# Two more Strassen units in the first up group of a one-layer decoder kernel, and another schedule for the early weight sums

## The chip, the core and the metric

The kernel runs on one core of one Trainium2 chip. The core has engines that work side by side, each through its own instructions in their order: PE (TensorE, matrix products), DVE (VectorE), ACT (ScalarE), POOL (GpSimd) and SP (SyncE), of which the last is used here to start DMA transfers. The metric is the device time of one execution in microseconds (us). A profile is one execution, recorded engine by engine.

## The reference

One decoder layer for 256 tokens of width 2048, in float32. Its matrix products set the time:

```
a = rmsnorm(h);  proj = a @ w_in                      # 2048 x 5184
... latent attention (8 heads), block attention (8 heads) ...
h = h + concat(out_mla, out_moba) @ w_o               # 2048 x 2048
f = rmsnorm(h)
h = h + (silu(f @ w_gate) * (f @ w_up)) @ w_down      # 2048 x 5632 twice, 5632 x 2048
h = h + sigmoid(rmsnorm(h) @ w_ple_gate) * (p @ w_ple_proj)
out = rmsnorm(h)
```

## The kernel before

**Units.** Every product is cut into *groups* of 1024 (or fewer) weight columns. A group is a list of *units*; a unit is a pair of 128-row tiles of the weight, some 1 MB. A unit's weight comes by DMA from SP's queue into one of five raw buffers (`load`, L213). It is then split: ACT casts it to the high part (`split_hi`, L345, the cast stands in L352), DVE subtracts the high part from the raw weight to get the low part (`split_lo`, L354, the subtraction in L363). High and low parts go into slots of 512 columns in a ring; the planner (`plan`, L247) gives each split its slots and so the turn of PE that must be past before they can be written. The pieces are called `ring`, `more` and `most`, by place. A product is three matmuls of 512 columns (`three`, L394): high by high, low by high, high by low. An ordinary unit has 2 row tiles, 2 column halves and 2 token tiles: 8 products, 24 matmuls.

**Strassen units.** In the feed-forward part most units (written `S0`, `S1`, ... in `mixed`, L1040) take a 2x2 scheme with 7 products, 21 matmuls (`seven`, L441). Such a unit is split in four pieces: "11 22" (1024 columns), "21" (512), "t1 t3" (1024) and "t4 t2" (1024), 3584 columns against 2048. The last two are sums of the weight's quarters. Usually DVE makes them in `split_lo`, with L362 ahead of the split of "21", and L365 and L366 behind it. After the last Strassen unit of a group DVE joins the partial results into a tile `U` (L464 to L468), for which the unit's second last product (m6 in its last turn) has to be done.

**Early sums.** For some units, marked `early`, the sums are made long before, in the attention part (`early_sums`, L368): POOL starts a DMA of the weight into a tile `wsums`, DVE makes the sums (L381 to L383) once PE's program has passed 38400 more matmul columns, and POOL starts a DMA that writes them to DRAM. The later `load` then fetches two quarters and "21" from the weight and the sums from DRAM, into two raw buffers, and DVE has only the four splits left for that unit. One tile serves all 12 sets. In `mixed` (L1048) g1 to g4 have one early unit each, u1 to u4 two each.

**Order.** The feed-forward part runs g0, u0, g1, d10, u1, d11, g2, ... (g is a gate group, u an up group, d a down group); with g0, u0 and g1 there is no down group between u0 and g1. u0 holds the row pairs `6 7 S0 S1 2 3 4 5`, g1 holds `6 S0 S1 S2 S3 S4 S5 7`. When an up group ends, DVE adds `U` to each of its four banks (L427) and multiplies by the gate (L1008); PE then turns the result by 16 transposes (`ff_transpose`, L1028), which stand in PE's program in the next gate group behind the first half of its first unit. `step` (L506) advances background tasks (attention heads, early sums) once per unit, the main loop (L1294) puts casts, splits and products in order. `v` is the group that makes the last columns of the value projection, `wo0` and `wo1` the output projection behind it.

Of the kernel before, what the change touches and what calls it, by code (L numbers as in the profile page):

```python
# [8 lines left out]
F32 = mybir.dt.float32  # L9
# [26 lines left out]
def kernel(ctx, tc, x, p, positions, attn_norm, w_in, kv_norm, w_ukv, w_o, ffn_norm,  # L36
# [6 lines left out]
    big = ctx.enter_context(tc.tile_pool(name="big", bufs=1))  # L43
# [24 lines left out]
    def load_x(dst, c0, c1):  # L68
        nc.sync.dma_start(dst[:, :, c0:c1], x_v[:, :, c0:c1])
# [114 lines left out]
    units = []  # L184
# [28 lines left out]
    def load(i):  # L213
        if i >= len(units) or units[i].again or i in raw:
            return
        u = units[i]
        u.asked = asking[0]
        while max(u.raw, u.raw2) >= len(raws):
            n = len(raws)
            raws.append(big.tile([128, 2048], F32, name=f"raw{n}", tag=f"f1{'hl'[n - 3]}"))  # L220
        if u.early:
            r = raws[u.raw][:, 0:1536]
            (w, c0, _), k0 = u.srcs[0], u.ks[0] * 128
            nc.sync.dma_start(r[:, 0:512], w[k0:k0 + 128, c0:c0 + 512])
            nc.sync.dma_start(r[:, 512:1536], w[k0 + 128:k0 + 256, c0:c0 + 1024])
            nc.sync.dma_start(raws[u.raw2], u.early)
            raw[i] = r.rearrange("q (a c) -> q a c", a=3)
            return
        n = sum(c1 - c0 for _, c0, c1 in u.srcs)
        nk = len(u.ks)  # L230
        r = raws[u.raw][:, 0:nk * n].rearrange("q (k c) -> q k c", k=nk)
        o = 0
        for w, c0, c1 in u.srcs:
            k0 = u.ks[0]
            nc.sync.dma_start(r[:, :, o:o + c1 - c0],
                              w[k0 * 128:(k0 + nk) * 128, c0:c1].rearrange("(k q) c -> q k c", q=128))
            o += c1 - c0
        raw[i] = r
# [126 lines left out]
            tt(f[:, 3], f[:, 3], f[:, 0], op=ALU.subtract)  # L365
            tt(f[:, 2], f[:, 2], f[:, 3], op=ALU.subtract)  # L366

    def early_sums():  # L368

        for u in units:  # L370
            if not u.early:
                continue
            f = big.tile([128, 4, 512], F32, name="wsums", tag="more_sums")
            (w, c0, _), k0 = u.srcs[0], u.ks[0] * 128
            nc.gpsimd.dma_start(f.rearrange("q (k a) c -> q k (a c)", k=2),
                                w[k0:k0 + 256, c0:c0 + 1024].rearrange("(k q) c -> q k c", q=128))
            since = columns[0]
            while columns[0] < since + 38400:
                yield 1
            tt = nc.vector.tensor_tensor  # L380
            tt(f[:, 0:2], f[:, 1:2].to_broadcast([128, 2, 512]), f[:, 0:4:3], op=ALU.subtract)  # L381
            tt(f[:, 3], f[:, 3], f[:, 0], op=ALU.subtract)
            tt(f[:, 2], f[:, 2], f[:, 3], op=ALU.subtract)  # L383
            u.early = dram.tile([128, 2048], F32, name=f"wsums{u.name}{u.idx}")
            nc.gpsimd.dma_start(u.early, f.rearrange("q a c -> q (a c)"))
# [6 lines left out]
    columns = [0]  # L392
# [110 lines left out]
    def add(gen, wait=0, front=False):  # L503
        tasks.insert(0 if front else len(tasks), [wait, gen])
# [143 lines left out]
    S = {"done": 0, "doneB": 0}  # L648
# [56 lines left out]
    def transpose_heads(src, col, n, dst):  # L705

        for i0 in range(0, n, 2):
            b = obank()
            for i in range(2):
                for t in range(NT):  # L710
                    nc.tensor.transpose(b[:, (2 * i + t) * 128:(2 * i + t + 1) * 128],  # L711
                                        src[:, t, col(i0 + i):col(i0 + i) + 128], ident)
            nc.scalar.copy(dst[:, i0:i0 + 2, :], b.rearrange("q (a s) -> q a s", a=2))
            yield 1
# [28 lines left out]
    def after_kv(half):  # L743
        def g():
            st = S["kv", half]
            qk = S["qk"]
            yield 1
            yield from transpose_heads(st, lambda i: i * 256, 4, qk[1][:, 4 * half:4 * half + 4])
            yield 1
            for i in range(4):  # L750
                add(head_mla(half, i), 0, True)
                yield 1
        add(g())
# [68 lines left out]

    def oM_alloc():
        S["oM"] = parts_tile("oM", "f0")
    oM_alloc()

    def ck_l(k, t):
        return lhs_of(S["ckvT"])(k, t)
# [208 lines left out]

    wg, wup, wd = w_gate[0], w_up[0], w_down[0]

    def mixed(name, order=((0, 0), (1, 0), (0, 1), (1, 1))):  # L1040

        pairs = {'g0': '0 1 2 3 4 5 6 7', 'u0': '6 7 S0 S1 2 3 4 5', 'g1': '6 S0 S1 S2 S3 S4 S5 7'}.get(
            name, '6 S0 S1 S2 S3 S4 S5 7' if name[0] == 'g' else 'S0 S1 S2 S3 S4 S5 S6 7').split()
        n = [int(x.strip("S+")) for x in pairs]
        sevens = tuple(i for i, x in enumerate(pairs) if x[0] == "S")
        return dict(ks=[2 * x + i for x in n for i in range(2)], chunks=C2, lhs=a_l, sums=a_sums, sevens=sevens,
                    adding=tuple(i for i, x in enumerate(pairs) if x[-1] == "+"),
                    early=sevens[-2 if name[0] == "u" else -1:] if name[-1] in "1234" else (), order=list(order) if sevens else None,  # L1048
                    swap=not sevens, deep=True)

    def gate(ci):
# [38 lines left out]
    for hc in range(2):  # L1090
        pairs = LAST[hc].split()
        group(f"dl{hc}", [(wd, hc * 1024, hc * 1024 + 1024)], [2 * int(x.strip("S")) + i for x in pairs for i in range(2)],
              C2, ff_l, add_evac(hc * 1024, ssp, norm_half(8 * hc, G_PLE, ssp if hc else None, "rp", 1 if hc else 6)),
              sevens=tuple(i for i, x in enumerate(pairs) if x[0] == "S"), sums=sum_at(LAST_SUMS, 8),
              order=[(0, 0), (1, 0), (0, 1), (1, 1)] if hc else None, deep=True, into=hc * 1024, swap=not hc)
# [141 lines left out]
    for n in range(3):  # L1237
        for i in range(4):
            if n:
                u = Unit()  # L1240
# [53 lines left out]
    for i, u in enumerate(units):  # L1294
        asking[0] = i
        if i < wide:
            load(i + 3)
        if u.name == "q0" and u.idx == 0:
            add(early_sums())
        if u.name == "g1" and u.idx == 0:  # L1300
            S["mid"] = S.pop("turned")
        if u.name == "wo0":
            S["twice"] = u.idx < 4
        if i < 5:
            load_x(xt, 768 + 256 * i, 1024 + 256 * i)
        if u.name == "dl0" and u.idx == 1:
            h_back()
        if u.name == "dl0" and u.idx == 0:
            add(sums_of(ffT[4], 32, LAST_SUMS, 8), 5)
        if u.name == "dl0" and u.idx == 2:  # L1310
            add(p_load())
        if u.name == "pg0" and u.idx == 0:
            fg_load()
        if u.name == "wo0" and u.idx < 4:
            step()
        for n in range(max(1, len(u.turns))):
            todo, late = [], []
            while i not in raw and u.turns:
                loads(i + 1)
            while nxt < len(jobs) and jobs[nxt].unit in raw and jobs[nxt].wait < j and jobs[nxt].unit <= i + (3 if i > 1 else 1) and \  # L1320
                    (jobs[nxt].unit <= i + 2 or i >= wide and units[jobs[nxt].unit].asked < i) and \
                    not (u.sevens_end and 0 <= n < 3 and jobs[nxt].unit > i + 1):
                todo.append(jobs[nxt])
                nxt += 1
            weave = u.name in WOVEN and u.last
            if "mid" in S and not u.strassen and u.mixed or u.sevens_end and n == 3 or weave:
                late = [jb for jb in todo if jb.turn > j]
                todo = [jb for jb in todo if jb.turn <= j]
            if i >= 5:
                high_parts(todo + late if weave else todo)  # L1330
            if i == 2:
                product(u, [0])
            if n % 2 == 0:
                step()
            for jb in todo:
                if i < 3:
                    for c0, c1 in units[jb.unit].chunks:
                        split_hi(jb, c0, c1, len(jb.kks))
                        split_lo(jb, c0, c1, len(jb.kks))
                    continue  # L1340
                split(jb)
            while posts:
                posts.pop()()
            if u.strassen:
                seven(u, n)
            elif i == 2:
                product(u, [1])
            else:
                product(u, [kk for jb in u.turns[n] for kk in jb.kks] if u.turns else range(len(u.ks)), late if weave else ())
            if "mid" in S and not u.strassen and u.mixed and 2 * u.idx + n >= 0 and len([*S["mid"]]) >= 0:  # L1350
                S.pop("mid")
            high_parts(late)
            for jb in late:
                split(jb)
            loads(len(units) if i >= wide else wide + 3)
            j += not u.again
# [25 lines left out]
```

## Time and profile before

| | us |
|---|---|
| median of 3 runs | 1189.46 |
| lowest and highest of the 3 | 1189.06, 1189.85 |
| the profiled execution, its own time | 1189.34 |
| its span, first to last instruction | 1187.6 |
| PE busy, DVE busy, ACT busy in it | 1175.0, 938.5, 708.4 |

The span is what the rows of the trace are placed in: their first number is the time from the span's start. The time of an execution is 1.74 us longer than its span. A row of the timeline gives the start, how long the instruction took, engine, line, operation, output and inputs, and in square brackets how long the engine stood idle before it and what released it. Matmuls overlap in the records: one is listed with 0.39 us, but the next starts 0.23 us later, so starts are what counts.

### The profile page before, as it was taken

Reading aid. Unit: us, or ns where it says so; the run is one execution under the profiler, and the core shown is the slowest. Engines: PE = TensorE matmul, PEld = TensorE weight load, DVE = VectorE, ACT = ScalarE, POOL = GpSimd, SP = SyncE. Lnnn points to the kernel's source line nnn. Section 1 sums busy time; section 2 is a strip of 40 time slices with the busy share of each in tenths; the row PEclk is TensorE's granted clock in tenths of the full one; section 3 lists DMA queues with packets and bytes.
Section 4 is the critical chain, followed back from the end, with each engine's and each line's share of the span. In section 5 each row is a group of like instructions: output and inputs, shape, how many; then the busy total and the mean of one; then the engine's idle time right before and its main releaser. Section 6 shows DMA issues by size and latency. Waiting matters only on the chain.

```text
span 1187.6 us, 14600 instructions
## 1 busy us (share of the span) xinstructions
PE 1175.0 (99%) x5486; PEld 982.7 (83%) x5486; DVE 938.5 (79%) x1109; ACT 708.4 (60%) x904; POOL 54.6 (5%) x76
## 2 busy tenths in 40 slices
PE   9999999999999999999999999999999999999996
PEld 7888888899888888888888888888888888888886
DVE  6656656766666678998999898989998999897474
ACT  6735745456555754566657575767575756465453
POOL 5200000000000000000000000000000000000000
PEclk9999999999999999999999999999999999999999
DMA  9775876667784776396978797778878795836631
GB/s 309 244 264 180 293 267 230 227 216 270 258 321 165 283 247 240 107 333 165 336 206 296 214 330 223 261 222 321 237 262 243 266 270 207 339 139 219 209 107 71
DMA packets 86647, 284.92 MB, mean 240 GB/s; under 512 B 5612, under 2 KB 10016, under 8 KB 82224
## 3 DMA queue, kind: packets, MB, share of 16 engines
q1 hardware_dynamic: 77664, 239.36, 56.9%
q0 software_dynamic: 8624, 44.10, 13.7%
q8 instruction: 43, 0.70, 0.2%
q10 hardware_dynamic: 288, 0.52, 0.1%
q14 instruction: 28, 0.23, 0.1%
HBM read 250.41 MB, written 25.17 MB: 232 GB/s over the span
## 4 chain that ended last, share of the span: by engine, by line
PE 90%; DVE 6%; ACT 2%; issue 1%; DMA 1%; ACTq 0%; POOL 0%; DVEq 0%; POOLq 0%
PE bank L399 29%; PE bank L397 28%; PE bank L398 28%; DVE ringl L363 2%; PE bank L138 1%; ACT ringh L352 1%; PE bank L1028 1%; DMA raw<-in_w_o 1%; DVE most L363 1%; PE bank L590 0%; DVE morel L363 0%; PE bank L619 0%; PE bank L593 0%; PE bank L711 0%; ACT att L603 0%
## 5 line engine op out<-in xcount | busy, mean ns | idle before, releaser
L352 ACT CAST ringh<-raw 128x1024 fp32r<-128x1024 f32 (+4 forms) x303 | 370.4, 1258 | 272.2 <-PE bank L398 123.6
L363 DVE TENSOR_TENSOR ringl<-raw,ringh 128x1024 fp32r<-128x1024 f32 (+4 forms) x301 | 436.5, 1473 | 108.2 <-ACT ringh L352 103.7
L397 PE MATMUL bank<-ringh,aT 128*128 128x512 f32 (+3 forms) x721 | 278.5, 386 | 0.0
L399 PE MATMUL bank<-ringl,aT 128*128 128x512 f32 (+3 forms) x721 | 273.6, 380 | 0.1
L398 PE MATMUL bank<-ringh,aT 128*128 128x512 f32 (+3 forms) x721 | 273.4, 379 | 0.0
L399 PEld LDWEIGHTS bank<-ringl,aT 128*128 128x128 f32 x721 | 135.5, 188 | 25.5 <-DVE ringl L363 0.7
L397 PEld LDWEIGHTS bank<-ringh,aT 128*128 128x128 f32 x721 | 135.8, 188 | 23.9 <-ACT aT L124 0.3
L398 PEld LDWEIGHTS bank<-ringh,aT 128*128 128x128 f32 x721 | 135.7, 188 | 23.7
L363 DVE TENSOR_TENSOR morel<-raw,moreh 128x1024 fp32r<-128x1024 f32 (+2 forms) x68 | 87.4, 1305 | 5.1 <-ACT moreh L352 4.5
L352 ACT CAST moreh<-raw 128x1024 fp32r<-128x1024 f32 (+2 forms) x70 | 77.6, 1143 | 21.1 <-DVE raw L362 11.4
L397 PE MATMUL bank<-ringh,ffTh 128*128 128x512 f32 x212 | 82.6, 389 | 0.0
L398 PE MATMUL bank<-ringh,ffTl 128*128 128x512 f32 x212 | 82.5, 389 | 0.0
L399 PE MATMUL bank<-ringl,ffTh 128*128 128x512 f32 x212 | 82.5, 389 | 0.0
L352 ACT CAST most<-raw 128x1024 fp32r<-128x1024 f32 (+2 forms) x58 | 57.7, 1021 | 37.2 <-DVE raw L362 16.4
L363 DVE TENSOR_TENSOR most<-raw,most 128x1024 fp32r<-128x1024 f32 (+2 forms) x58 | 67.6, 1182 | 1.3 <-ACT most L352 1.0
L362 DVE TENSOR_TENSOR raw<-raw 128x1024 f32<-128x1024 f32 x50 | 61.2, 1225 | 1.7
L398 PEld LDWEIGHTS bank<-ringh,ffTl 128*128 128x128 f32 x212 | 39.8, 188 | 8.3
L399 PEld LDWEIGHTS bank<-ringl,ffTh 128*128 128x128 f32 x212 | 39.8, 188 | 8.2
L397 PEld LDWEIGHTS bank<-ringh,ffTh 128*128 128x128 f32 x212 | 39.8, 188 | 8.2
L397 PE MATMUL bank<-moreh,aT 128*128 128x512 f32 x92 | 36.0, 391 | 0.0
L366 DVE TENSOR_TENSOR raw<-raw 128x512 f32<-128x512 f32 x50 | 34.6, 692 | 1.7
L399 PE MATMUL bank<-morel,aT 128*128 128x512 f32 x92 | 35.8, 389 | 0.0
(361 smaller groups left out, 1929.5 us busy)
## 6 DMA issues: line engine op xcount, KB each, us to landing
raw<-in_w_down SPq DMA_DIRECT2D x44, 1024.0 KB, 7.2
raw<-in_w_gate SPq DMA_DIRECT2D x36, 1024.0 KB, 7.2
raw<-in_w_up SPq DMA_DIRECT2D x32, 1024.0 KB, 7.8
raw<-in_w_in SPq DMA_DIRECT2D x40, 512.0 KB, 4.8
raw<-in_w_o SPq DMA_DIRECT2D x16, 1024.0 KB, 7.2
raw<-in_w_ple_gate SPq DMA_DIRECT2D x16, 1024.0 KB, 5.1
raw<-in_w_in SPq DMA_DIRECT2D x8, 1024.0 KB, 4.9
wsums<-in_w_up POOLq DMA_DIRECT2D x8, 1024.0 KB, 7.8
```

The source lines that it names most:

```text
L138: nc.tensor.transpose(b[:, (2 * i + t) * 128:(2 * i + t + 1) * 128], part[:, t, i * 128:(i + 1) * 128], ident)
L352: nc.scalar.copy(h[:, :, c0:c1], r[:, :, c0:c1])
L362: tt(f[:, 0:2], f[:, 1:2].to_broadcast([128, 2, 512]), f[:, 0:4:3], op=ALU.subtract)
L363: tt(l[:, :, c0:c1], r[:, :, c0:c1], h[:, :, c0:c1].bitcast(F32), op=ALU.subtract)
L366: tt(f[:, 2], f[:, 2], f[:, 3], op=ALU.subtract)
L397: nc.tensor.matmul(b, xh, h, start=start, stop=False)
L398: nc.tensor.matmul(b, xl, h, start=False, stop=False)
L399: nc.tensor.matmul(b, xh, l, start=False, stop=stop)
L1028: nc.tensor.transpose(b[:, (2 * i + t) * 128:(2 * i + t + 1) * 128], st[:, t, (k + i) * 128:(k + i + 1) * 128], ident)
```

## The change

It does four things.

- u0 takes the scheme for two more row pairs: `6 7 S0 S1 S2 S3 4 5`. The two new ones, S2 and S3, have early sums.
- Which units have early sums is now a table, `EARLY`: u0 2, g1 2, u1 2, g2 1, u2 2, g3 1, u3 2, g4 1, u4 1. So u0 gets two sets, g1 one more, u4 one less: 14 sets for 12.
- The sets are made by two chains at first. One begins in the first group (`ga`, its sixth unit) with a second tile in the slot `f0l`, for three sets; the other as before at the start of `q0`. The attention's output tile, which uses `f0l` later, is allocated only when the first four heads start.
- The wait between a set's DMA and DVE's sums is 34816 matmul columns, and no set is summed while the flag `crowded` is set: in the group `v` from its second unit, and in `wo0` up to its fourth.

```diff
-    def early_sums():
-
-        for u in units:
-            if not u.early:
-                continue
-            f = big.tile([128, 4, 512], F32, name="wsums", tag="more_sums")
+    todo_early = []
+
+    def early_sums(tag, enough=99):
+
+        made = 0
+        while todo_early and made < enough:
+            u = todo_early.pop(0)
+            made += 1
+            f = big.tile([128, 4, 512], F32, name="wsums", tag=tag)
             (w, c0, _), k0 = u.srcs[0], u.ks[0] * 128
             nc.gpsimd.dma_start(f.rearrange("q (k a) c -> q k (a c)", k=2),
                                 w[k0:k0 + 256, c0:c0 + 1024].rearrange("(k q) c -> q k c", q=128))
             since = columns[0]
-            while columns[0] < since + 38400:
+            while columns[0] < since + 34816 or S["crowded"]:
                 yield 1
...
+            if half == 0:
+                oM_alloc()
...
     def oM_alloc():
         S["oM"] = parts_tile("oM", "f0")
-    oM_alloc()
...
+    EARLY = dict(u0=2, g1=2, u1=2, g2=1, u2=2, g3=1, u3=2, g4=1, u4=1)
+
...
-        pairs = {'g0': '0 1 2 3 4 5 6 7', 'u0': '6 7 S0 S1 2 3 4 5', 'g1': '6 S0 S1 S2 S3 S4 S5 7'}.get(
+        pairs = {'g0': '0 1 2 3 4 5 6 7', 'u0': '6 7 S0 S1 S2 S3 4 5', 'g1': '6 S0 S1 S2 S3 S4 S5 7'}.get(
...
-                    early=sevens[-2 if name[0] == "u" else -1:] if name[-1] in "1234" else (), order=list(order) if sevens else None,
+                    early=sevens[-EARLY.get(name, 0):] if name in EARLY else (), order=list(order) if sevens else None,
...
+        S["crowded"] = u.name == "v" and u.idx > 0 or u.name == "wo0" and u.idx < 4
+        if u.name == "ga" and u.idx == 5:
+            todo_early.extend(x for x in units if x.early)
+            add(early_sums("f0l", 3))
         if u.name == "q0" and u.idx == 0:
-            add(early_sums())
+            add(early_sums("more_sums"))
```

**DVE between the join of u0's `U` and the first add at u0's end.** The first row of each piece is the join's last instruction, the last row the first bank's add. Before, raw_2910, raw_2912 and raw_112 are u0's units 3, 4 and 5, raw_113 is g1's first unit and raw_114 g1's S0:

```order
L468 TENSOR_TENSOR U<-U,bank_81 128x512
L363 TENSOR_TENSOR ringl<-raw_2910,ringh 128x1024 x2
L363 TENSOR_TENSOR morel<-raw_2912,moreh 128x1024 x2
L363 TENSOR_TENSOR most<-raw_112,most 128x1024 x2
L363 TENSOR_TENSOR ringl<-raw_113,ringh 128x1024 x2
L363 TENSOR_TENSOR ringl<-raw_114,ringh 128x1024
L362 TENSOR_TENSOR raw_114<-raw_114 128x1024
L363 TENSOR_TENSOR ringl<-raw_114,ringh 128x512
L365 TENSOR_TENSOR raw_114<-raw_114 128x512
L366 TENSOR_TENSOR raw_114<-raw_114 128x512
L363 TENSOR_TENSOR ringl<-raw_114,ringh 128x1024 x2
L427 TENSOR_TENSOR U<-U,bank_77 128x512
```

Now raw_114 is u0's unit 5, raw_2924 g1's first unit and raw_2926 g1's S0 (lines are those of the changed kernel):

```order
L471 TENSOR_TENSOR U<-U,bank_81 128x512
L363 TENSOR_TENSOR ringl<-raw_114,ringh 128x1024 x2
L363 TENSOR_TENSOR morel<-raw_2924,moreh 128x1024 x2
L363 TENSOR_TENSOR most<-raw_2926,most 128x1024
L362 TENSOR_TENSOR raw_2926<-raw_2926 128x1024
L363 TENSOR_TENSOR most<-raw_2926,most 128x512
L365 TENSOR_TENSOR raw_2926<-raw_2926 128x512
L366 TENSOR_TENSOR raw_2926<-raw_2926 128x512
L363 TENSOR_TENSOR ringl<-raw_2926,ringh 128x1024 x2
L430 TENSOR_TENSOR U<-U,bank_77 128x512
```

Two ordinary units' splits fewer stand between the join and the add: the join has moved two units nearer to the group's end, because the last Strassen unit has.

**PE around the transposes in g1.** Before, these rows stand where the first half of g1's first unit ends (bank_82 is its fourth bank) and the second begins:

```order
L399 MATMUL bank_82<-ringl,aT_85 128x512
L1028 MATMUL bank_77<-ident,stage 128x128 x4
L1028 MATMUL bank_78<-ident,stage 128x128 x4
L1028 MATMUL bank_79<-ident,stage 128x128 x4
L1028 MATMUL bank_80<-ident,stage 128x128 x4
L397 MATMUL bank_83<-ringh,aT_85 128x512
```

Now the same place reads:

```order
L402 MATMUL bank_82<-morel,aT_85 128x512
L1032 MATMUL bank_77<-ident,stage 128x128 x4
L1032 MATMUL bank_78<-ident,stage 128x128 x4
L1032 MATMUL bank_79<-ident,stage 128x128 x4
L1032 MATMUL bank_80<-ident,stage 128x128 x4
L400 MATMUL bank_83<-moreh,aT_85 128x512
```

The transposes have not moved; only the weight's slots differ.

**DVE in u4 around S5.** Before, raw_2912 is S4, raw_112 holds S5's quarters and raw_113 its sums; the last row is S6:

```order
L363 TENSOR_TENSOR most<-raw_2912,most 128x1024
L363 TENSOR_TENSOR ringl<-raw_2912,ringh 128x1024
L363 TENSOR_TENSOR ringl<-raw_112,ringh 128x1024
L363 TENSOR_TENSOR ringl<-raw_112,ringh 128x512
L363 TENSOR_TENSOR ringl<-raw_113,ringh 128x1024 x2
L363 TENSOR_TENSOR ringl<-raw_114,ringh 128x1024
```

Now raw_114 is S4, raw_2924 S5 and raw_2926 S6:

```order
L363 TENSOR_TENSOR most<-raw_114,most 128x1024
L363 TENSOR_TENSOR ringl<-raw_114,ringh 128x1024
L363 TENSOR_TENSOR ringl<-raw_2924,ringh 128x1024
L362 TENSOR_TENSOR raw_2924<-raw_2924 128x1024
L363 TENSOR_TENSOR ringl<-raw_2924,ringh 128x512
L365 TENSOR_TENSOR raw_2924<-raw_2924 128x512
L366 TENSOR_TENSOR raw_2924<-raw_2924 128x512
L363 TENSOR_TENSOR ringl<-raw_2924,ringh 128x1024 x2
L363 TENSOR_TENSOR ringl<-raw_2926,ringh 128x1024
```

The three sums of S5 stand in DVE's line again.

## The prediction

> **What bounds the kernel now.** I read the page's busy shares and chain first, then PE's waits, then timelines around the edited places.
>
> ```profile
> PE 1175.0 (99%) x5486; PEld 982.7 (83%) x5486; DVE 938.5 (79%) x1109; ACT 708.4 (60%) x904; POOL 54.6 (5%) x76
> ...
> PEclk9999999999999999999999999999999999999999
> ...
> PE 90%; DVE 6%; ACT 2%; issue 1%; DMA 1%; ACTq 0%; POOL 0%; DVEq 0%; POOLq 0%
> ```
>
> PE is busy in 99% of the span and carries 90% of the chain that ended last, at a full granted clock throughout. So a matmul taken away is time gained, unless PE then waits. All that it waits today:
>
> ```profile
> PE bank L113 <- DVE junk L108: 2.0, 1, 2.0
> PE bank L399 <- DVE most L363: 0.9, 1, 0.9
> PE bank L619 <- DVE att L596: 0.3, 1, 0.3
> PE bank L613 <- ACT att L609: 0.3, 1, 0.3
> ```
>
> The 2.0 is at the start. So at most 1.5 us of waiting is there to be removed, and what decides is which wait the change makes. The place to look is the timeline of PE in u0 and the head of g1:
>
> ```profile
> 443.20 0.39 PE L397 MATMUL bank<-ringh,aT 128*128 128x512 f32 x1
> ...
> 451.36 0.39 PE L397 MATMUL bank<-ringh,sumsatt 128*128 128x512 f32 x1
> ...
> 474.48 0.39 PE L397 MATMUL bank<-ringh,aT 128*128 128x512 f32 x1
> ...
> 477.20 1.91 PE L1028 MATMUL bank<-ident,stage 128*128 128x128 f32 x16
> 478.87 0.48 PE L397 MATMUL bank<-ringh,aT 128*128 128x512 f32 x1
> ```
>
> 443.20 is the start of u0's S0 and 474.48 that of g1. Between them stand two Strassen units (2 x 21 matmuls) and four ordinary ones (4 x 24): 138 matmuls in 31.28 us, **0.2267 us a matmul**, 4.76 us a Strassen unit, 5.44 us an ordinary one. The transposes stand 12 matmuls behind the start of g1 and last 1.67 us together (477.20 to 478.87). 451.36 is m6 of S1, the product on which the join of `U` waits; its three matmuls end 0.68 later.
>
> **The sum, part by part.** It is made against the profiled execution, 1189.34; the median lies 0.12 above that, so the two are interchangeable here.
>
> *Fewer matmuls.* Two ordinary units become Strassen units: 2 x 3 = 6 matmuls fewer, 6 x 0.2267 = **-1.36**.
>
> *The join and the transposes.* DVE in the same stretch:
>
> ```profile
> 452.31 0.69 DVE L465 TENSOR_TENSOR U<-U,bank 128x512 f32<-128x512 f32 x1 [3.38 <-ACT moreh L352]
> ...
> 454.95 1.22 DVE L363 TENSOR_TENSOR ringl<-raw,ringh 128x1024 fp32r<-128x1024 f32 x1
> ...
> 461.77 1.22 DVE L363 TENSOR_TENSOR ringl<-raw,ringh 128x1024 fp32r<-128x1024 f32 x1
> ...
> 475.40 0.75 DVE L1008 SCALAR_TENSOR_TENSOR stage<-U,rf,stage 128x512 f32<-128x512 f32 x1
> ...
> 476.79 0.75 DVE L1008 SCALAR_TENSOR_TENSOR stage<-U,rf,stage 128x512 f32<-128x512 f32 x1
> ```
>
> DVE idled 3.38 us and began the join at 452.31, which is 0.27 after m6 was done (451.36 + 0.68 = 452.04). The bracket names ACT, but m6 is what came last. From there DVE has no gap up to the last evacuation of the group: the join takes 2.64 (452.31 to 454.95), the splits of units 3, 4 and 5 take 2.27 each ((461.77 - 454.95) / 3), and from the start of the splits of g1's first unit (461.77) it is 14.38 us to the end of the third bank's evacuation (476.15) and 15.77 to that of the fourth (477.54). The transposes of the first two banks need the third, those of the last two the fourth. PE reached them at 477.20, so 1.05 us behind the third, and did not wait.
>
> After the change m6 is that of S3, two Strassen units later: 452.31 + 2 x 4.76 = 461.83. DVE's order shows the join in the same place behind m6's unit, and behind it now only unit 5 ahead of g1's first unit: 461.83 + 2.64 + 2.27 = 466.74. The third evacuation ends at 466.74 + 14.38 = 481.12, the fourth at 482.51. PE, from S0 at 443.20, comes to the transposes after 4 x 21 + 2 x 24 + 12 = 144 matmuls, at 475.84. It waits 5.28, does half the transposes in 0.83, and waits 482.51 - 481.95 = 0.56 more: **+5.84**. In short: between m6 and the transposes PE loses two ordinary units of work, 10.9 us, and DVE only their splits, 4.5. DVE's queue is served in order, so what stands behind the join can't fill the idle time ahead of it.
>
> *The stall in g1.*
>
> ```profile
> 502.99 0.39 PE L398 MATMUL bank<-most,sumsmore_sums 128*128 128x512 f32 x1
> 504.28 0.50 PE L399 MATMUL bank<-most,sumsmore_sums 128*128 128x512 f32 x1 [0.90 <-DVE most L363]
> ```
>
> Starts 1.29 apart instead of 0.2267: 1.06 us, because DVE is behind with S4's sums. S4 is now early, and PE arrives later after its wait: **-1.06**. Without the new wait the missing sums of S4 would do the same.
>
> *u4 has one set less.* S5's sums return to DVE's line.
>
> ```profile
> 465.29 1.23 DVE L362 TENSOR_TENSOR raw<-raw 128x1024 f32<-128x1024 f32 x1
> ...
> 468.36 1.22 DVE L363 TENSOR_TENSOR ringl<-raw,ringh 128x1024 fp32r<-128x1024 f32 x1
> ...
> 910.91 1.23 DVE L363 TENSOR_TENSOR ringl<-raw,ringh 128x1024 fp32r<-128x1024 f32 x1 [4.42 <-ACT ringh L352]
> ...
> 930.01 2.36 DVE L363 TENSOR_TENSOR ringl<-raw,ringh 128x1024 fp32r<-128x1024 f32 x2
> ...
> 935.44 0.39 PE L399 MATMUL bank<-ringl,sumsmore_sums 128*128 128x512 f32 x1
> ...
> 943.08 2.29 DVE L363 TENSOR_TENSOR ringl<-raw,ringh 128x2048 fp32r<-128x2048 f32 x1 [1.56 <-ACT ringh L352]
> ```
>
> The second split of the 930.01 row is S5's "11 22"; it ends at 932.37. Then come L362, "21", L365 and L366, 3.07 us in the pattern of 465.29 to 468.36, and the split of "t1 t3" from 935.44 to 936.66. PE wants that at 935.44: **+1.22**. Nothing ahead absorbs it, since DVE starts this stage level with PE (the idle 4.42 at 910.91, a wait for ring slots). Behind S5 the idle 1.56 at 943.08 takes up the rest. Bounds: 0, if DVE finds itself 1.2 ahead of what I read; 2.6, if all three sums of a set fall on PE.
>
> *The early part.* Sets and their transfers:
>
> ```profile
> L381 DVE TENSOR_TENSOR wsums<-wsums 128x1024 f32<-128x1024 f32 x12 | 14.6, 1215 | 0.0
> L383 DVE TENSOR_TENSOR wsums<-wsums 128x512 f32<-128x512 f32 x12 | 8.3, 692 | 0.4
> L382 DVE TENSOR_TENSOR wsums<-wsums 128x512 f32<-128x512 f32 x12 | 8.3, 692 | 0.4
> ...
> wsums<-in_w_up POOLq DMA_DIRECT2D x8, 1024.0 KB, 7.8
> ...
> 88.20 2.29 DVE L363 TENSOR_TENSOR ringl<-raw,ringh 128x2048 fp32r<-128x2048 f32 x1 [3.15 <-ACT ringh L352]
> ...
> 277.36 7.75 DMA raw<-in_w_o
> ```
>
> A set costs DVE 1.22 + 0.69 + 0.69 = 2.60. In the projection groups DVE idles some 3.15 in every 5.44 us unit (88.20), so the two extra sets, and the first ones earlier, are hidden at **0**. Two tiles can fall due together: 5.2 exceeds one gap by 2.05, and the ring, some units deep, covers that. The bounds are 0 and two such collisions uncovered, 4.1. A set's read lands in 7.8 us, and the new wait of 34816 columns (68 matmuls of 512, 15.4 us) leaves that room. In `v` the chain of waits runs through a set at 273.35, then waits for a `raw` at 277.36 (7.75) and ends in PE's two waits of 0.30 and 0.29. With `crowded` no set stands there, 2.6 us go, more than both: **-0.59**.
>
> *The clock in the wait.* What PE's clock does when PE stands still is seen only at the end:
>
> ```profile
> 1178.38 0.28 PE L399 MATMUL bank<-wfl,aT 128*128 128x256 f32 x1
> ...
> 1180.00:1182.00 2.00, 0.00 (x0) 0.00 (x0) 1.82 (x9) 0.87 (x3) 0.00 (x0) 0.99 0.00 0
> 1182.00:1183.00 1.00, 0.00 (x0) 0.00 (x0) 1.00 (x4) 0.69 (x1) 0.00 (x0) 0.50 0.00 0
> ```
>
> The last matmul ends at 1178.66, and the granted clock is 0.99 up to 1182 and 0.50 from there: 3.3 us of idle time drop it. The new wait is 5.28. If work brings the clock back as slowly as its absence took it, 3.3 us run at half speed and lose 1.65, part of it beneath the second wait of 0.56: I take **+1.0**, an estimate, with bounds 0 and 3.3.
>
> The Trainium skill, "TensorE: Matmul & The Clock Gate", section "Part 1: The HAM clock gate (the "warmup" mystery)", has the clock halve after an idle window of about 3.4 us whose phase runs free, and return after as much sustained work. By the page an idle time of 5.28 holds a whole window in some 55 of 100 phases, so the sum would be 1193.4 or about 1195; the end of this trace (3.3) agrees with its length and shows no phase.
>
> Sum: 1189.34 - 1.36 + 5.84 - 1.06 + 1.22 - 0.59 + 1.0 = **1194.4**.
>
> **The rivals.**
>
> *The clock stays open*: the wait is there, but the clock does not drop in it: 1194.4 - 1.0 = 1193.4. For it: 5.28 is not far above 3.3, and the clock was seen to drop once.
>
> *No wait at the transposes; faster.* The mechanism is DVE's place at the join. The splits of unit 5, g1's first unit and g1's S0 make up some 11 us (2.27 + 2.27 + 6.74); if 5.3 us of them or more are done ahead of the join, in DVE's idle time, the evacuations end before PE arrives. Then 1189.34 - 1.36 - 1.06 - 0.59 + 1.22 = 1187.6, and 1186.3 if u4's term goes too. Against it: the order rows put the join ahead of these splits, and an engine's queue is in order. It would take my reading of which product the join waits for to be wrong: were it one that is done some 5 us earlier, the result would turn.
>
> *The early sets collide.* With three sets in flight from the first group, pairs of 5.2 us stand in DVE's way (price 2.05 each beyond one gap, twice, less or more by the ring), or a set's write fills the transfers that the splits wait for: 1194.4 + 2.6 = 1197.0. Against it: DVE is 79% busy, less in that part, and a 3.15 gap in each unit refills.
>
> *The change doesn't do what it says*: the sums of S2 and S3 are late at 451.4 and 457.5, or the sets run past the attention, and PE waits in u0 itself: beyond 1197.
>
> **How the numbers follow.** Forecast 1194.4: 0.38. Clock stays open, 1193.4: 0.24. No wait, 1187.6: 0.17. Collision, 1197.0: 0.12. The rest, mostly beyond 1197, 0.09. The first two alone span 1192 to 1196.5 with their bounds (u4's 0 and 2.6, the clock's 3.3). To hold 8 in 10 the range has to take in the centre of the third and reaches to the fourth: 1187.6 to 1197.0. A measurement of this kernel can tell about 0.2%, 2.4 us: below 1187.1 is only the part of the third case with u4's term gone and something besides, 0.08; within 1187.1 to 1191.8 the rest of it and some of the second with small terms, 0.20; above, 0.72.
>
> **What would show it.** *Right:* a row of L1032, the transposes, near 476 with an idle time of 5 us or more released by DVE's `stage`, and DVE's join starting some 9.5 us later than before with a long idle time ahead of it; the stall of 0.90 in g1 and the waits of 0.30 and 0.29 gone; a new wait of about 1.2 in u4's S5; a granted clock below 1 behind the transposes. *Wrong:* the transposes run without a wait; the join starts before S3's m6; PE waits in u0 or in the projections; the difference of the two spans lies elsewhere than in these five places.

## The result, and the profile after

The changed kernel takes 1203.82 us (median of 4 runs, 1203.22 to 1205.53) against 1189.65 before in the same comparison: a ratio of 1.0123, 95% interval 1.0108 to 1.0138. Forecast were 1194.4, with a range that ended at 1197.0. It is slower, as forecast, but by 14.2 us and not by 5. Two slow runs (1994.29 us in e4 and, of the kernel before, 1308.49 us beside e5 to e8), at a granted clock of 0.56 and 0.85, are left out of the medians below.

The page's busy shares, granted clock and first figures of the chain, after:

```profile
PE 1177.6 (98%) x5480; PEld 984.5 (82%) x5480; DVE 948.7 (79%) x1119; ACT 713.7 (59%) x908; POOL 57.5 (5%) x80
...
PEclk9998999999999999899999999999999999999999
...
PE 90%; DVE 4%; issue 3%; DMA 2%; ACT 1%; POOL 0%; SPq 0%; DVEq 0%; ACTq 0%; POOLq 0%
```

The clock's row has an 8 in the fourth slice (90 to 120 us) and one in the seventeenth (481 to 511 us), where before there were none. Those are the two places of the loss. PE's waits, and then PE's own rows at the places:

```profile
PE bank L402 <- DVE ringl L363: 7.9, 2, 6.7
PE bank L1032 <- DVE stage L1012: 4.9, 2, 3.6
PE bank L113 <- DVE junk L108: 2.0, 1, 2.0
```

```profile
103.63 0.80 PE L402 MATMUL bank<-ringl,ckvT 128*128 128x512 f32 x1 [6.71 <-DVE ringl L363]
104.22 0.63 PE L400 MATMUL bank<-ringh,ckvT 128*128 128x512 f32 x1
104.65 0.63 PE L401 MATMUL bank<-ringh,ckvT 128*128 128x512 f32 x1
...
482.38 0.39 PE L402 MATMUL bank<-morel,aT 128*128 128x512 f32 x1
484.06 0.33 PE L1032 MATMUL bank<-ident,stage 128*128 128x128 f32 x1 [1.29 <-DVE stage L1012]
487.97 0.48 PE L1032 MATMUL bank<-ident,stage 128*128 128x128 f32 x1 [3.58 <-DVE stage L1012]
...
949.12 0.50 PE L402 MATMUL bank<-ringl,sumsmore_sums 128*128 128x512 f32 x1 [1.16 <-DVE ringl L363]
```

At 484 and 949 stand the two waits that were forecast. The one at 103.63, the longest, was not: it lies in the attention part, far from u0. Behind it the matmuls start 0.43 apart (104.22 to 104.65), which is half the clock.

PE runs matmuls of the same sizes in the same order in both kernels, but for the 6 that u0 lost, so each of PE's starts can be set beside its twin. The differences grow or shrink at a few places only. The next table has them, from the two profiled executions (1189.34 and 1203.47, 14.13 apart):

| place | after minus before, on arriving there | on leaving | change | forecast |
|---|---|---|---|---|
| first matmuls | 0 | -0.91 | -0.9 | 0 |
| attention part near 100 us | -0.91 | 8.28 | **+9.2** | **0** |
| attention part, 290 to 308 us | 8.28 | 6.75 | -1.5 | -0.6 |
| u0 | 6.75 | 5.41 | -1.3 | -1.4 |
| transposes in g1 and behind | 5.41 | 13.58 | +8.2 | +6.8 |
| g1's S4 | 13.58 | 12.36 | -1.22 | -1.06 |
| u4's S5 | 12.36 | 13.81 | +1.45 | +1.22 |

The first line is not of the change: other runs of kernels that begin alike stand between -1.0 and +0.3 there. Three lines (u0, S4, S5) lie within 0.25 of the forecast, and the attention part at 290 us and the transposes are off by 0.9 and 1.3. One, the second, is 9.2 where nothing was forecast. The last 0.3 of the 14.13 come behind PE's last matmul.

What stood in DVE's way near 100 us, in DVE's own rows (of a set's three sums the first; L363 is a split):

```profile
70.68 1.23 DVE L384 TENSOR_TENSOR wsums<-wsums 128x1024 f32<-128x1024 f32 x1 [0.47 <-DMA wsums<-in_w_gate]
...
81.91 2.29 DVE L363 TENSOR_TENSOR ringl<-raw,ringh 128x2048 fp32r<-128x2048 f32 x1 [3.10 <-ACT ringh L352]
88.74 1.22 DVE L384 TENSOR_TENSOR wsums<-wsums 128x1024 f32<-128x1024 f32 x1 [4.54 <-DMA wsums<-in_w_gate]
...
98.69 1.23 DVE L384 TENSOR_TENSOR wsums<-wsums 128x1024 f32<-128x1024 f32 x1 [7.28 <-DMA wsums<-in_w_up]
...
101.29 4.49 DVE L363 TENSOR_TENSOR ringl<-raw,ringh 128x2048 fp32r<-128x2048 f32 x2
```

DVE stood still 4.54 and 7.28 us for sets whose weights had not landed. The two sets belong to the two chains and stand right behind each other in DVE's queue, and the next splits stand behind both. So DVE makes no split from 84.20 (the end of the split of 81.91) to 101.29: 17.1 us, of which only 5.2 are sums. PE uses up a unit's splits in 5.44 us; it waits from 96.92. Why the weights were late is seen in POOL's rows, which issue the sets' reads (L378) and writes (L388):

```profile
60.33 0.71 POOL L378 DMA_DIRECT2D wsums<-in_w_up  x1 [4.18 <-DMA wsumsu<-wsums]
61.04 0.72 POOL L378 DMA_DIRECT2D wsums<-in_w_gate  x1
70.52 0.57 POOL L388 DMA_DIRECT2D wsumsu<-wsums  x1 [8.75 <-DVE wsums L386]
80.15 0.70 POOL L378 DMA_DIRECT2D wsums<-in_w_gate  x1 [9.07 <-DMA wsumsu<-wsums]
80.85 0.57 POOL L388 DMA_DIRECT2D wsumsg<-wsums  x1
91.84 0.70 POOL L378 DMA_DIRECT2D wsums<-in_w_up  x1 [10.42 <-DMA wsumsg<-wsums]
```

Both chains use the one queue of POOL. The first chain's write goes out at 70.52, and its next read waits 9.07 us until that write has landed and its tile is free. The second chain's write stands behind this read: its sums are done at 73.4 (the set of 70.68, 2.7 us of sums), but the write goes out only at 80.85. Its next read then waits 10.42 for that write, and is issued at 91.84. So 21.3 us pass between the first chain's write and the second chain's read, where 34816 columns give 15.4.

### The profile page after: what moved, and what is told of

It reads as the page before. It is cut to its first block, busy times and chain, and to the rows that moved or that the text cites. A ratio compares the mean times of both kernels' runs of the same rounds, so it can differ in the third digit from the quotient of the medians.

```text
span 1201.7 us, 14617 instructions
## 1 busy us (share of the span) xinstructions
PE 1177.6 (98%) x5480; PEld 984.5 (82%) x5480; DVE 948.7 (79%) x1119; ACT 713.7 (59%) x908; POOL 57.5 (5%) x80
## 4 chain that ended last, share of the span: by engine, by line
PE 90%; DVE 4%; issue 3%; DMA 2%; ACT 1%; POOL 0%; SPq 0%; DVEq 0%; ACTq 0%; POOLq 0%
PE bank L402 28%; PE bank L400 28%; PE bank L401 28%; DVE ringl L363 2%; DMA wsums<-in_w_up 1%; PE bank L1032 1%; ACT ringh L352 1%; PE bank L593 1%; PE bank L138 1%; PE bank L714 1%; PE bank L622 1%; PE bank L616 0%; PE bank L596 0%; DMA wsumsu<-wsums 0%; PE bank L623 0%
## 5 line engine op out<-in xcount | busy, mean ns | idle before, releaser
L363 DVE TENSOR_TENSOR ringl<-raw,ringh 128x1024 fp32r<-128x1024 f32 (+4 forms) x307 | 444.1, 1468 | 101.5 <-ACT ringh L352 99.2
L400 PE MATMUL bank<-ringh,aT 128*128 128x512 f32 (+3 forms) x713 | 274.8, 385 | 0.0
L402 PE MATMUL bank<-ringl,aT 128*128 128x512 f32 (+3 forms) x713 | 270.4, 379 | 0.0
L401 PE MATMUL bank<-ringh,aT 128*128 128x512 f32 (+3 forms) x713 | 270.1, 379 | 0.0
L401 PEld LDWEIGHTS bank<-ringh,aT 128*128 128x128 f32 x713 | 134.1, 188 | 23.4
L400 PEld LDWEIGHTS bank<-ringh,aT 128*128 128x128 f32 x713 | 134.0, 188 | 23.2
L363 DVE TENSOR_TENSOR morel<-raw,moreh 128x1024 fp32r<-128x1024 f32 (+2 forms) x66 | 85.5, 1317 | 1.4 <-ACT moreh L352 0.7
L400 PE MATMUL bank<-ringh,ffTh 128*128 128x512 f32 x204 | 79.4, 389 | 0.0
L401 PE MATMUL bank<-ringh,ffTl 128*128 128x512 f32 x204 | 79.4, 389 | 0.0
L402 PE MATMUL bank<-ringl,ffTh 128*128 128x512 f32 x204 | 79.4, 389 | 0.0
L363 DVE TENSOR_TENSOR most<-raw,most 128x1024 fp32r<-128x1024 f32 (+2 forms) x58 | 66.2, 1164 | 3.1 <-ACT most L352 3.1
L400 PE MATMUL bank<-most,aT 128*128 128x512 f32 x88 | 34.6, 393 | 0.0
L402 PE MATMUL bank<-most,aT 128*128 128x512 f32 x88 | 34.3, 389 | 0.0
```

What stands on the lines that cost most here:

```text
L363: tt(l[:, :, c0:c1], r[:, :, c0:c1], h[:, :, c0:c1].bitcast(F32), op=ALU.subtract)
L400: nc.tensor.matmul(b, xh, h, start=start, stop=False)
L401: nc.tensor.matmul(b, xl, h, start=False, stop=False)
L402: nc.tensor.matmul(b, xh, l, start=False, stop=stop)
```

## The experiments

Each is an edit of the changed kernel, and the time of the kernel before on the same chip stands beside it. The ledger is the one above: PE's starts against those of before.

**One chain, e1.**

```diff
         if u.name == "ga" and u.idx == 5:
             todo_early.extend(x for x in units if x.early)
-            add(early_sums("f0l", 3))
```

> Only the first chain of early sets (tile f0l, from the gate group's sixth unit of the attention part) is left out; all 14 sets are made by one chain from q0 on, with the same wait of 34816 columns. Theory Q (the 6.71 us wait at 103.63 and the half clock behind it come from two chains in POOL's one queue: a read stands behind the other chain's write): the wait goes, 6.9 us of waiting and 2.3 us of half clock, so 1203.8 - 9.2 = 1194.6 us. Rival C (34816 columns are too short a time for a set's transfers): a wait of DVE for a set's read stays, time above 1199. Rival T (two more sets of traffic): the waits move elsewhere, above 1199.

Measured: 1204.61 (before 1189.03; ratio 1.0130, 1.0114 to 1.0145). The total is as bad, but not for the same reason. Near 100 us nothing is lost any more. The loss has moved to the output projection. PE's row there, DVE's row ahead of it and POOL's write and read for that set:

```profile
346.21 0.76 PE L400 MATMUL bank<-ringh,oMh 128*128 128x512 f32 x1 [6.64 <-DVE h L899]
```

```profile
340.59 1.23 DVE L384 TENSOR_TENSOR wsums<-wsums 128x1024 f32<-128x1024 f32 x1 [7.81 <-DMA wsums<-in_w_up]
```

```profile
319.39 0.55 POOL L388 DMA_DIRECT2D wsumsu<-wsums  x1 [70.19 <-DVE wsums L386]
330.83 0.71 POOL L378 DMA_DIRECT2D wsums<-in_w_up  x1 [10.89 <-DMA wsumsu<-wsums]
```

A single chain that starts at q0 has ten sets out of the way at 243 us, then `crowded` stops it until 316, and four sets are left for the output projection and what follows. There a write took 10.89 until the next read could go, and DVE came to the sums 7.81 too early. A further 1.4 go at 384 us, where PE waits for ACT. Theory Q is right about the place near 100 us, wrong about the total; rival C is right for this place. Rival T, that the traffic of two more sets only moves the waits about, fits this run too; e4 and e5 bear on it.

**The join one unit earlier, e2.**

```diff
-        'u0': '6 7 S0 S1 S2 S3 4 5'
+        'u0': '6 S0 S1 S2 S3 7 4 5'
```

> u0's order is 6 S0 S1 S2 S3 7 4 5 instead of 6 7 S0 S1 S2 S3 4 5: the last Strassen unit, and so the join of U, one ordinary unit (5.44 us) nearer to the group's start; nothing else. Theory J (the wait at g1's transposes is set by the join's distance from the group's end): from u0's start the join begins at 24.1 us, the third evacuation ends 2.64 + 2.27 + 14.38 later at 43.4, PE arrives at 43.5: no wait there but about 0.4 for the fourth, no drop of the clock; 1203.8 - 8.15 + 0.4 = 1196.0 us. Rival D (DVE is simply overloaded in g1, wherever the join stands): the wait stays at 3 us or more, above 1200.

Measured: 1198.44 (before 1189.03; ratio 1.0082, 1.0065 to 1.0099). The transposes' rows:

```profile
484.21 1.09 PE L1032 MATMUL bank<-ident,stage 128*128 128x128 f32 x8 [0.94 <-DVE stage L1012]
485.60 0.98 PE L1032 MATMUL bank<-ident,stage 128*128 128x128 f32 x7 [0.29 <-DVE stage L1012]
```

Two waits of 0.94 and 0.29 in place of 1.29 and 3.58, and the clock stays full: the place costs 1.9 instead of 8.2. The expected 0.4 was too little by 1.5, and the wait near 100 us was 7.1 in this run, 0.4 longer than in the change's profile. Rival D falls: DVE has the same work, only the join has moved.

**The transposes half a unit later, e3.**

```diff
-            if "mid" in S and not u.strassen and u.mixed and 2 * u.idx + n >= 0 and ...
+            if "mid" in S and not u.strassen and u.mixed and 2 * u.idx + n >= (u.name == "g1") and ...
```

> In g1 the transposes stand behind the second half of its first unit, 12 matmuls (2.72 us) later; nothing else. Theory K (8.15 us are lost there: 5.25 of waiting, and 2.9 because the clock halves after an idle time of over 3.3): the idle time shrinks to about 2.2 and 0.6, the clock stays full, 1203.8 - 8.15 + 2.8 = 1198.4 us. Rival W (only the waiting counts, the clock follows anyway): 2.72 are saved, 1201.1 us.

Measured: 1206.86 (before 1189.03; ratio 1.0149, 1.0134 to 1.0165), 3 us worse than the change. PE's rows:

```profile
488.30 1.09 PE L1032 MATMUL bank<-ident,stage 128*128 128x128 f32 x8 [2.36 <-DVE stage L1012]
489.68 0.98 PE L1032 MATMUL bank<-ident,stage 128*128 128x128 f32 x7 [0.29 <-DVE stage L1012]
495.76 0.79 PE L400 MATMUL bank<-most,aT 128*128 128x512 f32 x1 [5.09 <-DVE ffTl L122]
```

The wait at the transposes did shrink to 2.36, close to the expected 2.2, and the clock did not drop there. But behind it stands a new wait of 5.09: S0, which now follows at once, needs a bank that the transposes wrote and that DVE must first split (L122), and DVE is late with that for the same reason. The edit moved the loss instead of removing it, and the clock dropped at the second wait.

**u0 as before, the new schedule of the sets kept, e4.**

```diff
-        'u0': '6 7 S0 S1 S2 S3 4 5'
+        'u0': '6 7 S0 S1 2 3 4 5'
-    EARLY = dict(u0=2, g1=2, ...)
+    EARLY = dict(g1=2, ...)
```

> u0 is as before (6 7 S0 S1 2 3 4 5, no early sets there, so 12 sets); the new schedule of the sets (two chains, 34816 columns, crowded, the table) stays. Theories Q and J: the wait at g1's transposes goes (-8.15), 6 matmuls come back (+1.36), the wait near 100 us stays: 1203.8 - 8.15 + 1.36 = 1197.0 us, 7.4 above the kernel before. Rival: if it was the number of sets (14) that made the wait near 100 us, it goes too: about 1187.9.

Measured: 1198.33 (before 1189.03; ratio 1.0078, 1.0062 to 1.0095). The transposes don't wait, and the wait near 100 us stays at 7.4 us with 12 sets as with 14. So it is not the number of sets. The time is 1.3 above the expected one; the ledger has 1.0 of it in a wait of 0.8 at 147 us.

**One chain from the gate group on, nothing held back, e5.**

```diff
-            while columns[0] < since + 34816 or S["crowded"]:
+            while columns[0] < since + 34816:
...
-            add(early_sums("f0l", 3))
-        if u.name == "q0" and u.idx == 0:
             add(early_sums("more_sums"))
```

> All 14 sets in one chain (tile more_sums) that begins at the gate group's sixth unit of the attention part, 34816 columns, and no crowded: nothing holds a set back in v and wo0. u0 as in the change. Theory Q2 (the two chains made the wait near 100 us; the late sets of e1 came from crowded, which pushed three of them into the output projection, where a set's read takes longer to be issued and to land): neither wait is there, the waits of 0.3 in the attention that crowded had removed (1.5 us in all) come back: 1203.8 - 9.2 + 1.5 = 1196.1 us. Rival C (34816 columns are too short for a set's write and read wherever they stand): DVE waits several us for a set's read somewhere and PE with it, 1200 or more.

Measured: 1198.85 (before 1189.36; ratio 1.0080, 1.0063 to 1.0097). All 14 sets are done at 317 us, with 34816 columns. Once DVE waits for a set's read (2.15 us at 241.7), and PE does not wait then. So 15.4 us is enough time for a chain that is alone and outside the output projection: rival C falls here. So does rival T of e1, since 14 sets are made and neither the wait near 100 us nor that in the output projection is there. The 2.7 us above the expected time have another place: the set at 287.82 stands ahead of the attention's work, and PE waits 2.54 for it.

**The Strassen units first, e6.**

```diff
-        'u0': '6 7 S0 S1 S2 S3 4 5'
+        'u0': 'S0 S1 S2 S3 4 5 6 7'
```

> u0's order is S0 S1 S2 S3 4 5 6 7, nothing else: the join of U begins 18.6 us behind u0's start, the third evacuation can end 41.3 behind it, PE reaches the transposes at 43.5. Theory J: no wait at the transposes at all, 1203.8 - 8.15 = 1195.7 us. Rival: four Strassen units at the head of u0 outrun DVE (S0 and S1 cost it 6.74 each against 4.76 of PE) or S2's sums come too late, and PE waits 2 us or more inside u0: 1198 or more.

Measured: 1196.78 (before 1189.36; ratio 1.0065, 1.0050 to 1.0080). No wait is left at the transposes and none came up inside u0; the place costs 0.5 in the ledger.

**Both, e7.** e5 and e6 in one kernel.

> e5 and e6 together. Theories Q2 and J: both losses are gone, they add: 1203.8 - 9.2 + 1.5 - 8.15 = 1188.0 us, 1.0 under the kernel before. Rival: one of the two losses only moves, 1191 or more.

Measured: 1192.36 (before 1189.36; ratio 1.0025, 1.0015 to 1.0034). Neither big loss is there, but the time is 4.4 above the expected one and so beyond the rival's 1191. The ledger has 3.5 of it between 250 and 320 us, where PE waits 2.56 at 292.77 as in e5 and here the clock drops as well, and 0.7 at the transposes.

**The second chain one unit later, e8.**

```diff
-        if u.name == "q0" and u.idx == 0:
+        if u.name == "q0" and u.idx == 1:
```

> Both chains stay; the second begins one unit (5.4 us) later, so that its sums don't fall due in the same step as the first one's; nothing else. Theory Q-order (a read of the second chain is late because it stands in POOL's queue behind the first chain's read, which waits for a write to land): the wait near 100 us falls under 2 us and the clock stays full, 1203.8 - 8 = 1196 us. Rival Q-time (two chains move more than can land in 34816 columns, whatever the order): PE still waits 4 us or more there, 1200 or more.

Measured: 1197.35 (before 1189.36; ratio 1.0067, 1.0052 to 1.0082). DVE's, PE's and POOL's rows:

```profile
89.82 1.23 DVE L384 TENSOR_TENSOR wsums<-wsums 128x1024 f32<-128x1024 f32 x1 [5.05 <-DMA wsums<-in_w_gate]
...
92.42 2.29 DVE L363 TENSOR_TENSOR ringl<-raw,ringh 128x2048 fp32r<-128x2048 f32 x1
100.08 1.23 DVE L384 TENSOR_TENSOR wsums<-wsums 128x1024 f32<-128x1024 f32 x1 [5.38 <-DMA wsums<-in_w_up]
...
102.68 2.29 DVE L363 TENSOR_TENSOR ringl<-raw,ringh 128x2048 fp32r<-128x2048 f32 x1
```

```profile
105.02 0.50 PE L402 MATMUL bank<-ringl,ckvT 128*128 128x512 f32 x1 [1.62 <-DVE ringl L363]
```

```profile
71.85 0.57 POOL L388 DMA_DIRECT2D wsumsu<-wsums  x1 [9.24 <-DVE wsums L386]
81.00 0.70 POOL L378 DMA_DIRECT2D wsums<-in_w_gate  x1 [8.59 <-DMA wsumsu<-wsums]
81.70 0.57 POOL L388 DMA_DIRECT2D wsumsg<-wsums  x1
93.15 0.70 POOL L378 DMA_DIRECT2D wsums<-in_w_up  x1 [10.89 <-DMA wsumsg<-wsums]
```

With the same two chains and the same columns, the second one unit later, PE waits 1.62 in place of 6.71 and the clock stays full there. By the ledger the loss up to 150 us is 3.7 in place of 9.2, and 1.5 of it is another wait, for ACT at 141 us. But it is not POOL's queue that changed: the second chain's write still stands behind the first chain's read, again 21.3 us pass from the first chain's write to the second chain's read (71.85 to 93.15), and DVE still waits some 5 us twice. What changed is DVE's queue: a unit's splits (92.42) now stand between the two sets, so that the longest time without a split is 8.0 us (94.71 to 102.68) in place of 17.1. The expected wait came out, but not by the order in POOL's queue, which this edit leaves as it was: theory Q-order is not tested here. Rival Q-time falls by its number, PE's 4 us, though DVE's two waits are of its kind.

**A version that takes what was learned, e9, and its twin with the old u0, e10.**

```diff
-            while columns[0] < since + 34816 or S["crowded"]:
+            while columns[0] < since + (34816 if made < 13 else 69632) or S["crowded"]:
-    EARLY = dict(u0=2, g1=2, ...)
+    EARLY = dict(u0=2, g1=1, ...)
-        'u0': '6 7 S0 S1 S2 S3 4 5'
+        'u0': 'S0 S1 S2 S3 4 5 6 7'
-            add(early_sums("f0l", 3))
-        if u.name == "q0" and u.idx == 0:
             add(early_sums("more_sums"))
```

> u0 is S0 S1 S2 S3 4 5 6 7 with its two early sets; 13 sets (g1 one, not two) in one chain that begins at the gate group's sixth unit, 34816 columns, crowded as in the change, 69632 columns for the last set, so that its read has time behind the value group. Theories Q2 and J: no loss near 100 us, none in wo0, none at the transposes. From the profiled execution of before, 1189.34: -1.36 (6 matmuls) - 1.5 (the attention waits that crowded removes) + 1.16 (u4's S5); g1's S4 stall stays: 1187.6 us. Rival: one of the losses is left in part, 1190 or more.

> As e9, but u0 is 6 7 S0 S1 2 3 4 5 as in the kernel before, with 12 sets (none for u0, two for u4). What e9 gains over it is the worth of the two Strassen units themselves: -1.36 + 1.16 = -0.2. Expected: 1189.34 - 1.5 = 1187.8 us. Rival: the two units cost or bring more than that where nothing else stands in their way, a difference to e9 of over 1 us.

Measured, 11 runs each: e9 1188.07 (before 1189.23; ratio 0.9989, 0.9980 to 0.9998), e10 1187.90 (ratio 0.9987, 0.9978 to 0.9996). Both are faster than the kernel before by little, 1.2 and 1.3 us, both by what the schedule of the sets does in the attention part (some -1.55 in each ledger). PE's waits in e9:

```profile
PE bank L113 <- DVE junk L108: 2.0, 1, 2.0
PE bank L402 <- DVE ringl L363: 1.9, 2, 1.1
PE bank L138 <- DMA x<-in_x: 0.9, 1, 0.9
```

The 1.9 is g1's S4 and u4's S5; the first and the last row are at the kernel's start. Between e9 and e10 there are 0.17 us, within their spread: what the two Strassen units gain (1.32 in the ledger) and what the set that u4 gave up costs (1.46) cancel out.

## Why the prediction was wrong

- **The step that failed** is the one on the early part: "A set's read lands in 7.8 us, and the new wait of 34816 columns (68 matmuls of 512, 15.4 us) leaves that room", and so the sets were "hidden at **0**". It measured +9.2: 6.9 of standing and 2.3 behind it at half the clock. Two things in the step were wrong. It counted one read from the moment it is asked for. Between two sums of a chain lie a write and a read, and with two chains on one queue a write of the one stood behind a read of the other that waited for a tile; so DVE stood still 4.54 and 7.28 us. And it let two sets that fall due together cost DVE their own 5.2 us, which the ring would cover; with the two waits in it the pair kept DVE from splitting for 17.1 us. That the two chains make the loss is shown: e1, e5 and e9, with one chain, lose nothing there, and e4, with two chains and 12 sets, loses as much. That the pair standing together is most of it is borne out by e8, where with a unit's splits between the two sets PE's wait falls from 6.71 to 1.62 while POOL's queue is as before. How much the order in POOL's queue adds to the lateness of the weights is read from the rows and was not tried by itself. The rival "the early sets collide" named the place and the pair, but priced only DVE's own time for the sums (2.05 and 2.6), not DVE standing still for a set's transfer.
- **The join and the transposes:** the mechanism was right, and so were its times. The join began 18.65 us behind u0's S0 (468.60 after; S0 at 449.95, by the ledger), forecast 18.63; the third evacuation ended at 487.91 (487.16 + 0.75), 38.0 behind S0, forecast 37.9. PE's standing at the first two transposes amounts to 5.25 in the ledger (1.45 and 3.80) against 5.28 forecast. e2 and e6 show that the join's place sets it.
- **The clock in that wait** was mis-sized: 2.9 us behind the wait, 1.0 forecast (bounds 0 and 3.3). The half clock lasted longer than the idle time that caused it; the section on the hardware has the length. The forecast let a second wait of 0.56 cover part; there is no second wait, because the first eight transposes ran at half speed meanwhile.
- **The attention waits** that `crowded` removes: -1.5 against -0.59. The forecast took the two listed idle times, 0.30 and 0.29; by PE's starts they cost 0.46 each, and the few matmuls right behind them came another 0.10 and 0.54 late. e10 has the same -1.55 in its ledger without any change to u0.
- **Fewer matmuls, g1's S4, u4's S5:** -1.34, -1.22 and +1.45 against -1.36, -1.06 and +1.22. The forecast of the two stalls counted one late start each; the matmul behind it starts 0.11 or 0.12 late as well. The last is there, 1.45 to 1.8, in each experiment that kept one set for u4.
- **Whether the change can pay:** in e9 its two losses are gone, and the two Strassen units are worth nothing over e10. Their gain, 1.32 in the ledger, comes with two early sets; one of these is taken from u4 here, at 1.46.

What stays open: why a write of 1 MB took 9 to 11 us near 70, 80 and 320 us until the next read went, where most took 4 to 5. A read of the other chain was in flight beside the one of 80.85; beside those of 70.52 and, in e1, of 319.39 there was none. A longer wait in columns with both chains kept was not tried, nor a queue of its own for each chain.

## What to carry to other kernels

A wait that is counted in work of another engine has to hold the whole round trip of a buffer (write out, landing, read in, landing), on the queue as it is with its other users, and in the stage with the slowest transfers: one round trip is not two interleaved. Two such chains should not fall due in the same step either, since their waits then follow each other in the queue that serves both. When a product is moved later in a group, count the work of each engine between the two points that it ties together; the engine with less work left becomes the one that is waited for. And when a loss vanishes at one place, look for it at the next before taking the total as a verdict: e1 removed what it was made to remove and e3 more than half of it, yet e1 came out no faster than the change and e3 slower.

## What the runs showed of the hardware

The clock fell for spells of one length or a multiple of it. The windows behind the wait near 100 us in the changed kernel, where the last three columns are granted clock, DMA share and GB/s:

```profile
100.00:102.00 2.00, 0.00 (x0) 0.00 (x0) 1.97 (x3) 0.00 (x0) 0.34 (x1) 0.86 0.10 41
102.00:104.00 2.00, 0.37 (x1) 0.37 (x2) 2.00 (x2) 0.00 (x0) 0.22 (x1) 0.50 0.62 262
104.00:106.00 2.00, 2.00 (x6) 1.52 (x6) 2.00 (x3) 0.00 (x0) 0.00 (x0) 0.50 0.97 302
106.00:108.00 2.00, 2.00 (x6) 1.59 (x5) 1.83 (x8) 0.00 (x0) 0.71 (x1) 0.50 0.84 244
108.00:110.00 2.00, 2.00 (x10) 1.60 (x9) 1.93 (x5) 1.05 (x1) 0.00 (x0) 0.94 0.97 354
```

The shares missing from a full clock add up to 0.28 + 1.00 + 1.00 + 1.00 + 0.12 = 3.4 us, so 6.8 us at one half. Behind the transposes it was 6.8 as well; in e1, for the wait of 6.64, the missing shares add up to 5.1, so 10.2 us. The same sum in e7, for the wait of 2.56:

```profile
293.00:294.00 1.00, 1.00 (x7) 0.86 (x7) 0.97 (x4) 0.93 (x5) 0.00 (x0) 1.00 1.07 401
294.00:295.00 1.00, 1.00 (x4) 0.80 (x3) 0.93 (x3) 1.00 (x2) 0.00 (x0) 0.56 0.81 217
295.00:296.00 1.00, 1.00 (x3) 0.73 (x3) 0.69 (x3) 1.00 (x2) 0.70 (x1) 0.50 1.00 356
296.00:297.00 1.00, 1.00 (x4) 0.80 (x3) 0.00 (x0) 1.00 (x6) 0.00 (x0) 0.50 0.97 336
297.00:298.00 1.00, 1.00 (x5) 0.82 (x4) 0.00 (x0) 1.00 (x6) 0.00 (x0) 0.74 1.01 299
```

0.44 + 0.50 + 0.50 + 0.26 = 1.7, so 3.4 us at one half: half as long a spell. The clock fell 1.4 us after PE had gone on working, and for an idle time of 2.56. In e5 the same wait of 2.54 at the same place left the clock full, and so did 2.36 in e3.

The Trainium skill, "TensorE: Matmul & The Clock Gate", section "Part 1: The HAM clock gate (the "warmup" mystery)", has the activity judged in free-running windows of about 3.4 us. The lengths here, one, two and three times 3.4, and the two outcomes of one wait agree with that. It puts the fall behind at least one idle window; e7 fell for an idle time shorter than a window, so there the measurement decides.
